# A hybrid attention layer in two halves of the tokens: top-k search and sparse attention of the second half placed beside the MLP of the first

## The chip, the cores and the metric

The kernel runs on one core of one Trainium2 chip. The metric is the device time of one execution in microseconds (us). Engines: PE is TensorE, DVE is VectorE, ACT is ScalarE, POOL is GpSimd; SP issues most of the DMAs.

## The reference

One layer over 1024 tokens of width 1024, all in float32. Two groups of heads read one projection; their outputs are normed, concatenated and projected, and an MLP follows.

```
mod = silu(c) @ w_mod + b_mod                    # six vectors sh1, sc1, ga1, sh2, sc2, ga2
h = rmsnorm(x, g_attn) * (1 + sc1) + sh1
proj = h @ w_in                                  # split into the parts below
o_a = stick_breaking_attention(q_a, k_a, v_a)    # 8 heads of 64, strictly causal
o_b = dsa_attention(...)                         # 8 heads over a shared latent of 128
x = x + ga1 * (concat(rmsnorm(o_a), rmsnorm(o_b)) @ w_out)
h = rmsnorm(x, g_mlp) * (1 + sc2) + sh2
x = x + ga2 * (square(relu(h @ w_up)) @ w_down)  # 1024 -> 4096 -> 1024
out = rmsnorm(x, g_final)
```

Stick-breaking weighs key s for query t by beta_ts times the product of (1 - beta_tj) over s < j < t, with beta a sigmoid of the scores. The sparse heads first score all admissible keys with an indexer (8 small heads, relu, weighted sum), keep the 256 best of each query, and take a softmax over these with a position bias. A query sees the keys of its own chunk of 64 and of earlier ones, so the first half of the tokens needs nothing of the second.

## The kernel before, in words

All tiles have 128 partitions; the tokens are 8 blocks of 128 (two halves of 4), and block b has 128 (b + 1) keys. Every float32 matmul of precision is done as three: each operand is split into a rounded high part and the rest (`split`, L155 to L160; for weights `load_split`, L162 to L175: DMA, scale by a gate on DVE in L172 where there is one, high part on ACT in L173, rest on POOL in L174), and `mm3` (L177) issues L178, L179 and L180 for it. Most PE work stands under these three lines, whatever it belongs to; the tile names tell it apart.

The program is written in one order, but each engine's queue is laid out before the run by a planner: it simulates the engines and takes, for each one, the ready instruction that comes first in the program (`early` moves a call up or down by the offsets in `PRI`), if a buffer of its pool is free. Buffers are named by tags with a count; a tile waits for the last reader of the one whose place it takes.

The stages, in program order:

- x is loaded, normed and transposed; the first modulation vectors come from w_mod (L289); h is made as 32 half tiles hh and hl in the pool `hpool`, which has 32 places (L314).
- The indexer (L430 to L467) leaves the scores sc of blocks 2 to 7. Blocks 0 and 1 have no more than 256 keys and need no search.
- The search finds the 256th largest score of each row bit by bit, 32 steps (L538). Blocks 2 to 6 step together on DVE: a count for each block (L503 on the upper 16 bits, L529 on the lower 16) and two small operations that close the step. Block 7 counts on ACT (Sign with a sum, L552), with two small operations on DVE. Then one mask per block (`topk_mask`, L561 to L582; five passes of its width, L578 to L582) is made in bfloat16.
- The stick-breaking heads run in four pairs, 8 steps a pair (L860): a step is one head and two blocks of queries. `sb_weights` (L698) makes scores (L380, L381), two Sigmoids (L707, L708), a scan on DVE (L709) and a product on POOL (L711). `av_pair` (L610) transposes the weights (L621, L623), copies and splits them (L626 to L632), multiplies them with the values (L644, 256 columns) and adds the two halves of the result (L662). In each step the lists TK, MS and DQ say how many search steps, modulation pieces (`mod_piece`, L388: weights of w_mod, one multiply-add on DVE each, L402) and halves of the projection dq (`dq_half`, L766) are put in; the search begins ahead of the first pair and all masks are done by the end of the last.
- The sparse heads (L1059): 8 heads by 4 pairs of blocks. `ds_weights` (L790) makes the logits dz with mm3 and adds the mask by a matmul (L809), reduces them with the bias on DVE (L812), takes Exp on ACT with a sum (L816), and scales by the reciprocal on ACT, POOL or DVE (L819, L821, L823). `ds_finish` is `av_pair` again. The norm of the stick-breaking output and part of that of the sparse one are put in between (L918 to L965).
- The output projection (`out_tile`, L982) has w_out whole in 16 tiles and runs token block by token block; `h2_pair` (L1005) makes the MLP's input h2h and h2l from two token blocks. Ten modulation pieces stand here too (`MW`).
- The MLP (L1106): 8 groups of 4 slices of w_up; for each slice both halves of the tokens go through `up` (24 matmuls of 512 columns per half), Relu on ACT (L1119), square on DVE (L1120) and split (L159, L160); then `dn` over the 8 token blocks and 2 column halves (12 matmuls each), added to x1 on DVE (L1138). The last group ends in the final norm (L1143 to L1150).

The two lines that count in the search, and the two activations of the two kinds of heads:

```
V.tensor_scalar(jk[:, :widths[b]], src or sc[b], t, 0.5 - TOPK, op0=op, op1=OP.add, accum_out=c)        # L503
V.tensor_scalar(jk[:, :widths[b]], mk[b].bitcast(U16), tlo[:, j:j + 1], above[:, j:j + 1],
                op0=OP.is_ge, op1=OP.add, accum_out=cnt[0][:, j:j + 1])                                 # L529
A.activation(m[:, cs], z, AF.Sigmoid, scale=-0.125)                                                     # L707
A.activation(l, l, AF.Exp, bias=mx, scale=-1.0, accum_out=st[:, 0:1])                                   # L816
```

Of the kernel before, what the change touches and what calls it, by code (L numbers as in the profile page):

```python
# [1 line left out]

# [16 lines left out]
P = 128  # L19
# [13 lines left out]
TKB = ((2, 3, 4, 5, 6), (7,))  # L33
TK0 = 1
OTB = 1
DEPTH = 2
TRB = 3
AVB = 1
ZB = 4
ZO = 1  # L40
NA = (0, 1)
DQ2 = [0] * 32
MACB = 2
KTG = ((0, 1), (1, 3), (3, 5), (5, 7), (7, 8))
PMK = ()
PRI = {'tk': 0, 'mod': -100, 'proj': 50, 'dq': 0, 'v': 100, 'sw': 0, 'sf': 400, 'dw': -200, 'df': 0, 'kv': -200, 'ld': 0, 'na': 0, 'wo': -50, 'vb': 0, 'mt': 0, 'ht': 0, 'fp': 0, 'pb': 0, 'h2': 0}
HFD = (6, 7)
HLD = ((0, 1), (2, 0), (2, 1), (3, 1), (4, 0), (4, 1), (5, 1), (7, 0))
IKD = ()
TRA = (4,)  # L50
WL = 4
WS = 4
QK = 6
VA = 5
WT = 4
KL = 3
WHB = 2
WLB = 2
WRB = 2
LPS = ((1, 0), (1, 2), (2, 2), (3, 4))  # L60
LPD = ()
AVL = 0
FPOS = 'wfvsdtm'
SBO = (2, 0, 3, 1)
DSO = (3, 2, 1, 0)
SCP = (2, 6)
OTP = False
WOR = (1, 3, 6, 7)
WOV = (0,)
MW = [6, 1, 1, 5]  # L70
WOA = ((7, 3, 0), (6, 3, 1), (6, 3, 2))
DSL = 0
NBK = 0
PS_ACT = (1, 2)
PS_POOL = (0, 2, 3, 5, 6, 7)
MI = [4, 0, 5, 0, 2, 0, 0, 5]
# [8 lines left out]
def tile_trunk(ctx: ExitStack, tc: tile.TileContext, x, w_mod, w_in, w_uv, w_out, w_up, w_down,  # L85
# [76 lines left out]
    def load_split(shape, src, name, hi_tag=None, lo_tag=None, raw_tag=None, scale=None, lo_eng=None):  # L162

        hp_, ht, hb = hi_tag or (wp, "wh", WHB)
        lp_, lt, lb = lo_tag or (wp, "wl", WLB)
        rp_, rt, rb_ = raw_tag or (wp, "wr", WRB)
# [24 lines left out]
    DVE_BLOCKS, ACT_BLOCKS = TKB  # L191
    hTh, hTl = {}, {}
    widths = {b: P * (b + 1) for b in range(NB)}
    with ExitStack() as pctx:
        bp = pctx.enter_context(tc.tile_pool(name="bpool", bufs=1))
        pp = pctx.enter_context(tc.tile_pool(name="psb", bufs=1, space=PSUM))

        def ztile(name):
            return pp.tile([P, 512], F32, tag="z", bufs=ZB, name=name)

        def pjtile(name):
            return pp.tile([P, 512], F32, tag="tr", bufs=TRB, name=name)

        def trtile(name):
            return pp.tile([P, 512], F32, tag="tr", bufs=TRB, name=name)

        def avtile(name):
            return pp.tile([P, 512], F32, tag="av", bufs=AVB, name=name)

        def big(name, dt=F32):  # L210
            return bp.tile([P, S], dt, tag="wkL", bufs=WL, name=name)

        def wktile(name, n):
            if n > 512:
                return big(name)
            return bp.tile([P, 512], F32, tag="wkS", bufs=WS, name=name)

        def qktile(name):
            return bp.tile([P, S], F32R, tag="qk", bufs=QK, name=name)

        def kltile(name):
            return bp.tile([P, S], F32R, tag="kl", bufs=KL, name=name)

        def vtile(name):
            return bp.tile([P, 2, 4, P], F32R, tag="va", bufs=VA, name=name)
# [20 lines left out]
        for tt in range(8):  # L246
            xt = big(f"x{tt}") if tt < 4 else bp.tile([P, S], F32, tag="va", bufs=VA, name=f"x{tt}")
# [16 lines left out]
        for hf in range(2):  # L264
            for t4 in range(4):
# [3 lines left out]
                jk = bp.tile([P, D], mybir.dt.uint8, tag="jka", bufs=1, name=f"xjk{tt}")  # L269
# [19 lines left out]
        def mod_tiles(k0, k1):  # L289
            n = k1 - k0  # L290
            acc = bp.tile([P, 2, n * P], F32, tag="wt", bufs=WT, name=f"macc{k0}")
            ps = trtile(f"pm{k0}")
            for k in range(KT):
                r = raws[k0, k][:, 0:2, :]
                if k0 in PMK:
                    continue
# [4 lines left out]
            for s_ in range(2):  # L301
                for j in range(n):
                    if k0 in PMK:
                        for k in range(KT):
                            T.matmul(ps[:, n * s_ + j:n * s_ + j + 1], raws[k0, k][:, s_, j * P:(j + 1) * P],
                                     c_act[:, k:k + 1], start=k == 0, stop=k == KT - 1)
                        continue
# [890 lines left out]
```

## Time and profile before

| | us |
|---|---|
| median of 3 runs | 1624.12 (1624.05 to 1626.75) |
| the profiled execution, its own time | 1625.42 |
| its span, first to last instruction | 1623.6 |
| mean granted clock of TensorE | 0.948 of full |
| PE, DVE, ACT, POOL busy | 1468.8, 990.5, 667.6, 567.5 |
| moved by DMA | 121.49 MB |

A row of a group reads: line, engine, operation, out<-in by the program's names (buffer numbers left out), shapes, count | busy us, mean ns of one | idle time of the engine just before these and what ended most of it. Matmuls are pipelined: the duration of one reaches into the next, so their mean is no price and a busy PE is not a full one. "+4 forms" says that shapes of other sizes are in the group. Stretches are us from the start of the span.

### The profile page before, as it was taken

The numbers are of one execution on the slowest core, as the hardware profiler recorded it, in microseconds if no ns is written. First come the engines' busy times: TensorE is split into PE (matmuls) and PEld (weight loads), VectorE is DVE, ScalarE is ACT, GpSimd is POOL, SyncE is SP. The second block draws the span as 40 slices with busy tenths as digits, with TensorE's granted clock in tenths as the row PEclk, the third lists the DMA queues.
The fourth block names the chain that finished last, engine by engine and source line by source line (L and its number), as shares of the span: only waits on it lengthen the run. The fifth ranks groups of instructions, "written<-read, shape, count | busy, mean of one in ns | idle before, by whom it ended". The sixth has DMA issues, their size and how long they took to land.

```text
span 1623.6 us, 19672 instructions
## 1 busy us (share of the span) xinstructions
PE 1468.8 (90%) x7248; PEld 1213.9 (75%) x7248; DVE 990.5 (61%) x1842; ACT 667.6 (41%) x1258; POOL 567.5 (35%) x389
## 2 busy tenths in 40 slices
PE   4888867887798778999999899999999999999998
PEld 3668746666587657878778688888888888888886
DVE  7888999999957885999763542323333332323234
ACT  5775565433445545988632330303031212212032
POOL 4343123433436556675552330403031222213021
PEclk8999979888899879999999999999999999999999
DMA  9531211322111212211342530202021111202012
GB/s 324 150 105 28 78 46 39 105 64 91 34 40 40 68 55 85 91 59 53 117 143 101 208 94 0 92 13 78 26 65 40 53 52 39 66 27 78 6 34 104
DMA packets 103232, 121.49 MB, mean 75 GB/s; under 512 B 7856, under 2 KB 75480, under 8 KB 103136
## 3 DMA queue, kind: packets, MB, share of 16 engines
q1 hardware_dynamic: 102704, 120.20, 23.7%
q8 instruction: 57, 0.93, 0.3%
q14 instruction: 39, 0.32, 0.1%
q10 hardware_dynamic: 432, 0.03, 0.0%
HBM read 99.75 MB, written 16.27 MB: 71 GB/s over the span
## 4 chain that ended last, share of the span: by engine, by line
PE 61%; DVE 27%; issue 4%; ACT 3%; DMA 3%; POOL 1%; SPq 0%; DVEq 0%; POOLq 0%; ACTq 0%
PE up L178 7%; PE up L180 7%; PE up L179 7%; PE dn L178 7%; PE dn L179 7%; PE dn L180 7%; DVE tk_jk L503 4%; DVE tk_jk L529 4%; DVE m L709 4%; DVE m2acc L402 2%; DMA wm<-in_w_mod_dram 2%; PE wo L178 2%; PE wo L179 1%; PE wo L180 1%; PE avd L644 1%
## 5 line engine op out<-in xcount | busy, mean ns | idle before, releaser
L174 POOL TENSOR_TENSOR wld<-wrd,whd 128x1024 fp32r<-128x1024 f32 x32 | 77.3, 2415 | 474.5 <-ACT whd L173 474.5
L1138 DVE TENSOR_TENSOR x<-dn,x 128x512 f32<-128x512 f32 x128 | 87.7, 691 | 206.7 <-PE dn L180 206.7
L1119 ACT ACTIVATE r<-up 128x512 f32<-128x512 f32 x64 | 37.8, 591 | 402.7 <-PE up L180 402.7
L178 PE MATMUL up<-h2h,whup 128*128 128x512 f32 x512 | 200.0, 391 | 3.2 <-ACT h2f L1020 3.2
L179 PE MATMUL up<-h2l,whup 128*128 128x512 f32 x512 | 199.7, 390 | 0.0
L180 PE MATMUL up<-h2h,wlup 128*128 128x512 f32 x512 | 199.7, 390 | 0.0
L179 PE MATMUL dn<-wld,uh 128*128 128x512 f32 x512 | 199.2, 389 | 0.0
L180 PE MATMUL dn<-whd,ul 128*128 128x512 f32 x512 | 199.2, 389 | 0.0
L178 PE MATMUL dn<-whd,uh 128*128 128x512 f32 x512 | 196.6, 389 | 0.0
L1120 DVE SCALAR_TENSOR_TENSOR r<-up,r 128x512 f32<-128x512 f32 x64 | 44.3, 692 | 196.7 <-ACT r L1119 196.7
L711 POOL TENSOR_TENSOR be<-be,m 128x895 f32<-128x895 f32 (+7 forms) x64 | 89.5, 1401 | 170.0 <-DVE m L709 114.8
L709 DVE TENSOR_TENSOR_SCAN m<-m 128x896 f32<-128x896 f32 (+7 forms) x64 | 98.7, 1548 | 27.7 <-ACT m L707 25.3
L178 PEld LDWEIGHTS up<-h2h,whup 128*128 128x128 f32 x512 | 96.5, 188 | 23.5 <-ACT h2f L1020 3.5
L179 PEld LDWEIGHTS up<-h2l,whup 128*128 128x128 f32 x512 | 96.5, 189 | 20.1
L180 PEld LDWEIGHTS up<-h2h,wlup 128*128 128x128 f32 x512 | 96.4, 188 | 20.1
L178 PEld LDWEIGHTS dn<-whd,uh 128*128 128x128 f32 x512 | 96.1, 188 | 20.0
L180 PEld LDWEIGHTS dn<-whd,ul 128*128 128x128 f32 x512 | 96.1, 188 | 20.0
L179 PEld LDWEIGHTS dn<-wld,uh 128*128 128x128 f32 x512 | 96.1, 188 | 19.9
L174 POOL TENSOR_TENSOR wlup<-wrup,whup 128x1024 fp32r<-128x1024 f32 x32 | 77.1, 2408 | 27.3 <-ACT whup L173 27.2
L160 DVE TENSOR_TENSOR ul<-r,uh 128x512 fp32r<-128x512 f32 x64 | 57.2, 894 | 44.7 <-ACT uh L159 44.7
L529 DVE TENSOR_SCALAR_CACHE_REDUCE tk_jk<-mk,tlo,above 128x384 bf16<-128x384 uint16 (+4 forms) x80 | 74.7, 933 | 2.0
L644 PE MATMUL avs<-wts,va 128*128 128x256 f32 (+1 forms) x320 | 56.5, 306 | 16.4 <-DVE ota L662 7.3
(328 smaller groups left out, 3705.5 us busy)
## 6 DMA issues: line engine op xcount, KB each, us to landing
m2raw<-in_w_mod_dram SPq DMA_DIRECT2D x32, 512.0 KB, 4.4
wrup<-in_w_up_dram SPq DMA_DIRECT2D x32, 512.0 KB, 3.9
wrd<-in_w_down_dram SPq DMA_DIRECT2D x32, 512.0 KB, 3.4
wm<-in_w_mod_dram SPq DMA_DIRECT2D x24, 256.0 KB, 6.0
x<-in_x_dram SPq DMA_DIRECT2D x8, 512.0 KB, 6.2
wrdq<-in_w_in_dram SPq DMA_DIRECT2D x8, 512.0 KB, 3.7
dq<-dqf SPq DMA_DIRECT2D x16, 256.0 KB, 2.2
dqr<-dq SPq DMA_DIRECT2D x8, 512.0 KB
```

What stands on the lines that cost most here:

```text
L160: (lo_eng or V).tensor_tensor(lo, src, hi.bitcast(F32), op=OP.subtract)
L174: (lo_eng or G).tensor_tensor(lo, raw, hi.bitcast(F32), op=OP.subtract)
L178: T.matmul(ps, ah, bh, start=start, stop=False)
L179: T.matmul(ps, ah, bl, start=False, stop=False)
L180: T.matmul(ps, al, bh, start=False, stop=stop)
L503: V.tensor_scalar(jk[:, :widths[b]], src or sc[b], t, 0.5 - TOPK, op0=op, op1=OP.add, accum_out=c)
L529: V.tensor_scalar(jk[:, :widths[b]], mk[b].bitcast(U16), tlo[:, j:j + 1], above[:, j:j + 1], op0=OP.is_ge, op1=OP.add, accum_out=cnt[0][:, ...
L644: T.matmul(dst, vv, rhs, start=kt == 0 and l == 0, stop=half and l == 1)
L709: V.tensor_tensor_scan(m[:, :n][:, ::-1], m[:, :n][:, ::-1], m[:, :n][:, ::-1], 1.0, op0=OP.mult, op1=OP.bypass)
L711: G.tensor_tensor(be[:, :n - 1], be[:, :n - 1], m[:, 1:n], op=OP.mult)
L1120: V.scalar_tensor_tensor(r, ps, 0.0, r, op0=OP.max, op1=OP.mult)
L1138: V.tensor_tensor(x1[tt][:, cs], ps, x1[tt][:, cs], op=OP.add)
```

## The change

The program order after the change: the indexer as before; then the search in two groups on DVE, blocks 2 and 3 first, then blocks 4, 5 and 6 (block 7 on ACT as before). While the stick-breaking heads run, the lists TK and TA put in 51 of the 71 steps of the two groups (all of the first, and 16 of the second) and the 32 bit steps of block 7. The projections dq and kv are all done in the first three pairs; in the last pair the sparse heads of the first half (blocks 0 to 3) are put in, by the list D0, two steps to each stick-breaking step, their tiles in the places that hh and hl leave. All modulation pieces are done by then. A new set of pools is opened, with 3 + 2 + 1 + 2 places in PSUM for scores, transposes, the weighted values and the MLP (before: 4 + 3 + 1). Then come the norm and output projection of the first half, and its MLP as a generator of 97 pieces: 2 of them, then one after each step left of the search, then four after each of 18 steps of the second half's sparse heads. Then the norm, output projection and MLP of the second half alone, with the up matmuls one group ahead of the down matmuls. The weights w_up, w_down, w_out and w_uv are loaded and split once for each half; in the first half's MLP w_down is split in pieces of 512 columns.

Its core:

```diff
-TKB = ((2, 3, 4, 5, 6), (7,))
...
-MS = [2, 0, 1, 2, 2, 1, 1, 1, 1, 1, 0, 1, 1, 0, 0, 0, 0, 0, 0, 0, 0, 0, 0, 0, 0, 0, 0, 0, 0, 0, 0, 0]
-DQ = [1, 1, 1, 1, 1, 2, 0, 2, 0, 1, 1, 1, 0, 0, 0, 0, 0, 0, 0, 0, 0, 0, 0, 1, 0, 0, 1, 0, 1, 0, 1, 0]
-TK = [1, 1, 2, 1, 1, 2, 0, 2, 2, 1, 4, 0, 4, 0, 2, 0, 1, 2, 4, 3, 0, 0, 1, 0, 2, 1, 1, 1, 0, 0, 0, 3]
+GROUPS = ((2, 3), (4, 5, 6))
+ACT_BLOCK = 7
...
+MS = [2, 0, 1, 2, 2, 1, 1, 1, 1, 1, 0, 1, 1, 0, 0, 0, 1, 0, 1, 0, 1, 0, 1, 0, 1, 1, 1, 1, 1, 1, 0, 0]
+DQ = [1, 1, 1, 1, 1, 2, 0, 2, 0, 1, 1, 1, 0, 0, 1, 1, 0, 0, 1, 1, 0, 0, 0, 0]
+TK = [2, 2, 2, 2, 2, 2, 2, 2, 2, 2, 2, 2, 2, 2, 2, 2, 2, 1, 1, 1, 1, 1, 1, 1, 1, 1, 1, 1, 1, 1, 1, 1]
+TA = [1] * 32
+D0 = [3, 2, 2, 2, 2, 2, 2, 3]
+FILL_0, FILL_T, FILL_D = 2, 1, 4
...
+        def ds_steps(hf):
...
+            yield first
+            for h in range(8):
+                for i in (2 * hf + 1, 2 * hf):
+                    yield lambda h=h, i=i: step(h, i)
+            yield lambda: [ds_finish(*t) for t in todo]
...
+        tk, ta = chain(*[search(g) for g in GROUPS]), search_act(ACT_BLOCK)
+        run(tk, 2)
...
+        d0 = ds_steps(0)
         for pr in range(4):
...
-                            early("tk", topk_some, TK[8 * pr + k])
+                            run(tk, TK[8 * pr + k])
+                            run(ta, TA[8 * pr + k])
...
+                    if pr == 3:
+                        run(d0, D0[k])
                     k += 1
         sb_finish(*pending)
-        topk_some(99)
-        while left() > 10:
+        run(d0, 99)
+        while left():
             mod_some(1)
...
+        pctx.close()
+        pctx = ExitStack()
+        bp = pctx.enter_context(tc.tile_pool(name="dpool", bufs=1, reuse_waits="tile"))
+        pp = pctx.enter_context(tc.tile_pool(name="psd", bufs=1, space=PSUM, reuse_waits="tile"))
...
+        def up_tile(ft, hf, ps, r, uh, ul, lo_eng=None):
+            wuh, wul = load_split([P, KT, P], wu[:, :, ft * P:(ft + 1) * P], f"up{ft}_{hf}")
+            for kt in range(KT):
+                mm3(ps, wuh[:, kt, :], wul[:, kt, :], h2h[kt, hf], h2l[kt, hf], kt == 0, kt == KT - 1)
+            A.activation(r, ps, AF.Relu)
+            V.scalar_tensor_tensor(r, ps, 0.0, r, op0=OP.max, op1=OP.mult)
+            split(uh, ul, r, None, lo_eng)
...
+            def dn(fg, t, ch):
+                ps = mtile(f"dn{fg}_{t}_{ch}")
+                ts = slice(t * P, (t + 1) * P)
+                for f in range(FFG):
+                    mm3(ps, uh[f][:, ts], ul[f][:, ts], *wd[f, ch], f == 0, f == FFG - 1)
+                V.tensor_tensor(x1[t, ch], ps, x1[t, ch], op=OP.add)
...
+            yield begin
+            for fg in range(NG):
+                for f in range(FFG):
+                    yield lambda fg=fg, f=f: up(fg, f)
+                for ch in range(2):
+                    for t in range(4):
+                        yield lambda fg=fg, t=t, ch=ch: dn(fg, t, ch)
+
+        norm(0, 0)
+        norm(0, 1)
+        out_half(0)
+        m = mlp_beside()
+        run(m, FILL_0)
+        for _ in range(40):
+            n0 = len(seen)
+            run(tk, 1)
+            run(ta, 1)
+            if len(seen) == n0:
+                break
+            run(m, FILL_T)
+        d = ds_steps(1)
+        for _ in range(18):
+            run(d, 1)
+            run(m, FILL_D)
+        norm(1, 0)
+        run(m, 200)
+        norm(1, 1)
+        out_half(1)
...
+        up_group(0)
+        for fg in range(NG):
+            if fg < NG - 1:
+                up_group(fg + 1)
```

`search` and `search_act` hold the operations of `topk_step` and `topk_mask` as generators, `run` takes the next steps of one, `norm` and `out_half` hold those of the norms and of `out_tile` for one half, and `up_group` calls `up_tile` for four slices of the second half.

## Rows read from the trace of the kernel before

**Rows 1.** The page, part 1: busy us of each engine, share of the span, instructions.
```profile
PE 1468.8 (90%) x7248; PEld 1213.9 (75%) x7248; DVE 990.5 (61%) x1842; ACT 667.6 (41%) x1258; POOL 567.5 (35%) x389
```

**Rows 2.** Busy time by stage: stretch, length, each engine's busy us (instructions), granted clock, DMA share, GB/s.
```profile
158.00:226.00 68.00, 55.16 (x271) 44.40 (x269) 66.80 (x176) 38.24 (x64) 11.65 (x5) 0.89 0.27 72
226.00:640.00 414.00, 336.29 (x1735) 278.81 (x1736) 354.44 (x575) 201.40 (x418) 183.57 (x117) 0.87 0.20 60
640.00:826.00 186.00, 172.12 (x1179) 147.72 (x1178) 155.55 (x516) 146.47 (x319) 116.26 (x86) 0.98 0.23 78
826.00:918.40 92.40, 85.63 (x398) 67.11 (x396) 46.44 (x90) 31.12 (x61) 34.19 (x42) 1.00 0.39 127
918.40:1623.60 705.20, 698.08 (x3072) 577.57 (x3072) 239.87 (x311) 149.13 (x222) 159.30 (x90) 1.00 0.18 58
```

**Rows 3.** The chain of waits, in order of time: start us, us, what.
```profile
670.46 1.50 PE avd L644 x12
...
860.13 1.31 PE x2T L1014 x12
```

**Rows 4.** Groups of PE from 226 to 640 us: count, busy us, mean ns, idle before.
```profile
L644 PE MATMUL avs<-wts,va 128*128 128x256 f32 (+1 forms) x292 | 52.7, 308 | 16.4 <-DVE ota L662 7.3 <-DVE wts L632 7.1 <-POOL wts L630 1.5
L178 PE MATMUL dq<-hh,whdq 128*128 128x512 f32 x120 | 50.5, 421 | 4.5 <-DVE qo L371 3.9 <-ACT wfs L629 0.4 <-DVE wts L632 0.2
...
L623 PE MATMUL trs<-ident,be 128*128 128x128 f32 x153 | 39.5, 309 | 2.7 <-POOL be L711 2.7
L621 PE MATMUL trs<-ident,be 128*128 128x128 f32 x123 | 36.3, 315 | 30.1 <-DVE modT L418 16.0 <-DVE wts L632 6.5 <-ACT wfs L629 5.4
L178 PE MATMUL k<-hh,whk 128*128 128x512 f32 x48 | 22.2, 463 | 1.0 <-ACT wfs L629 0.5 <-DVE lo L690 0.5
...
L178 PE MATMUL q<-hh,whq 128*128 128x512 f32 x40 | 16.9, 423 | 0.0
```

**Rows 5.** Groups of PE from 640 to 826 us.
```profile
L644 PE MATMUL avd<-wtd,vb 128*128 128x256 f32 (+1 forms) x317 | 47.9, 287 | 4.1 <-ACT wtd L626 2.2 <-DVE otb L662 1.1 <-DVE wtd L632 0.3
L178 PE MATMUL dz<-kvh,dqh 128*128 128x384 f32 (+4 forms) x94 | 37.8, 403 | 4.2 <-DVE dst L812 3.0 <-DVE dst L817 1.1
L623 PE MATMUL trd<-ident,dl 128*128 128x128 f32 x160 | 35.2, 274 | 0.0
L621 PE MATMUL trd<-ident,dl 128*128 128x128 f32 x128 | 33.0, 282 | 4.2 <-DVE wtd L632 3.1 <-DVE of L937 0.9
...
L178 PE MATMUL wo<-who,oh 128*128 128x512 f32 x24 | 9.9, 440 | 0.0
```

**Rows 6.** Busy time of two stretches of the stick-breaking stage, columns as in rows 2.
```profile
200.00:440.00 240.00, 184.99 (x848) 147.48 (x846) 235.36 (x484) 115.26 (x231) 78.18 (x51) 0.84 0.23 67
440.00:520.00 80.00, 71.68 (x459) 63.71 (x459) 52.06 (x70) 42.77 (x90) 40.35 (x24) 0.93 0.15 42
```

**Rows 7.** Groups of VectorE from 158 to 640 us.
```profile
L529 DVE TENSOR_SCALAR_CACHE_REDUCE tk_jk<-mk,tlo,above 128x384 bf16<-128x384 uint16 (+4 forms) x80 | 74.7, 933 | 2.0
...
L402 DVE SCALAR_TENSOR_TENSOR m2acc<-m2raw,c_act,m2acc 128x512 f32<-128x512 f32 x20 | 17.0, 848 | 0.0
L579 DVE TENSOR_TENSOR_SCAN cs<-eq 128x384 f32<-128x384 f32 (+5 forms) x6 | 13.3, 2210 | 2.8 <-POOL be L711 2.8
...
L581 DVE SCALAR_TENSOR_TENSOR cs<-sc,thr,cs 128x384 f32<-128x384 f32 (+5 forms) x6 | 8.1, 1342 | 0.1
L580 DVE SCALAR_TENSOR_TENSOR cs<-cs,cnt,eq 128x384 f32<-128x384 f32 (+5 forms) x6 | 7.8, 1308 | 0.1
L582 DVE TENSOR_SCALAR mk<-cs 128x384 bf16<-128x384 f32 (+5 forms) x6 | 7.2, 1194 | 0.0
L578 DVE TENSOR_SCALAR eq<-sc,thr 128x384 f32<-128x384 f32 (+5 forms) x6 | 6.7, 1122 | 0.0
```

**Rows 8.** ScalarE in order of time, 642 to 644 us.
```profile
642.40 1.28 ACT L816 ACT_TABLE_LOAD   x1
643.75 1.04 ACT L816 ACTIVATE dl<-dl,dst 128x896 f32<-128x896 f32 x1
```

More of the change, by code (lines that the diff above doesn't have):

```diff
@@ L1 @@
 from contextlib import ExitStack
+from itertools import chain
 import concourse.bass as bass
@@ L392, in mod_piece @@
             acc = macc2[c]
-            rp_, rt, rb_ = (bp, "va", VA) if c < 6 else (wp, "wr", WRB)
-            raw = rp_.tile([P, 2, 512], F32, tag=rt, bufs=rb_, name=f"m2raw{c}_{k2}")
-            SY.dma_start(raw, wm[:, 2 * k2:2 * k2 + 2, c0:c0 + 512])
+            if late:
+                raw = [hp.tile([P, 512], F32, tag="h", name=f"m2raw{c}_{k2}_{u}") for u in range(2)]
+                for u in range(2):
+                    SY.dma_start(raw[u], wm[:, 2 * k2 + u, c0:c0 + 512])
+            else:
+                both = bp.tile([P, 2, 512], F32, tag="va", bufs=bf["va"], name=f"m2raw{c}_{k2}")
+                SY.dma_start(both, wm[:, 2 * k2:2 * k2 + 2, c0:c0 + 512])
+                raw = [both[:, u, :] for u in range(2)]
             for u in range(2):
@@ L433, in tile_trunk @@
         done = []
+        late = []
         def left():
@@ L586, in tile_trunk, with run, htile @@
+        seen = []
+        def run(it, n):
+            for _ in range(n):
+                s_ = next(it, None)
+                if s_:
+                    seen.append(1)
+                    s_()
+        def htile(name, dt=F32R):
+            return hp.tile([P, 512], dt, tag="h", name=name)
         va = {}
@@ L883, in tile_trunk @@
                         elif what == "d":
-                            for _ in range(DQ[8 * pr + k]):
-                                n_ = next(dqi, None)
-                                if n_ is not None:
-                                    early("dq", dq_half, n_ // 2, n_ % 2)
-                    if pr == 3 and k in (2, 4):
-                        if k == 2:
+                            for _ in range(DQ[8 * pr + k] if pr < 3 else 0):
+                                q_ = next(dqi, None)
+                                if q_ is not None:
+                                    early("dq", dq_half, q_ // 2, q_ % 2)
@@ new lines, in tile_trunk, with norm @@
+        V.scalar_tensor_tensor(A2, modT[:, 32:40], 1.0, gmT, op0=OP.add, op1=OP.mult)
+        oh_, ol_, of_ = {}, {}, {}
+        def norm(hf, part):
+            kts = range(4 * part, 4 * part + 4)
+            sqs = []
+            for kt in kts:
+                of_[kt, hf] = htile(f"of{kt}_{hf}", F32)
+                SY.dma_start(of_[kt, hf], scr[kt][:, hf * 512:(hf + 1) * 512])
+                sq = wktile(f"sq{kt}_{hf}", 512) if kt % 4 else htile(f"sq{kt}_{hf}", F32)
+                A.activation(sq, of_[kt, hf], AF.Square)
+                if sqs:
+                    G.tensor_tensor(sqs[0], sqs[0], sq, op=OP.add)
+                else:
+                    sqs.append(sq)
+            st = bp.tile([P, 4], F32, tag="nst", bufs=2, name=f"nst{hf}_{part}")
+            row_rstd1(pjtile(f"ss{hf}_{part}"), sqs, 512, st)
+            rs = pjtile(f"rs{hf}_{part}")
+            row_rstd2(rs, 4, st)
+            for kt in kts:
@@ L1005, in h2_pair @@
+                split(oh_[kt, hf], ol_[kt, hf], raw, A, G)
+        h2h, h2l = {}, {}
         def h2_pair(i, xs):
@@ L1094, in tile_trunk @@
+        mctx.close()
     with ExitStack() as pctx:
```

680 lines of the change are left out of this document (294 added, 386 removed).

## The prediction

> **What bounds it now.** I read the page's first part, then busy time by stage, then the groups of instructions inside a stage, then the chain of waits, and last ScalarE's order of time around one spot. The first part says PE 90% [rows 1], which looks like a kernel with nothing left. The stages say otherwise [rows 2]. From 918.4 us on (the MLP), 3072 matmuls of 512 columns keep PE busy 698.1 us: 0.227 us each, back to back. Before that a busy PE is not a full one. The chain shows what the other kinds cost when nothing holds them: 12 matmuls of mostly 256 columns in 1.50 us (0.125 each), 12 transposes in 1.31 us (0.109 each) [rows 3]. With these prices I turn counts into dense PE time. For 226 to 640 us (stick-breaking heads): dq, k and q are 120 + 48 + 40 matmuls on each of the three lines of mm3, 624 x 0.227 = 142; avs 292, a fifth of them half as wide, 33; 153 + 123 transposes 30 [rows 4]; v, kv and the scores, counted in the same way, 71: 276 us of dense work in 414 us, 67%. For 640 to 826 us (sparse heads): avd 36, dz 3 x 94 of mean 384 columns (0.172) 48, 160 + 128 transposes 31, vb and masks 13, so 128, and 72 first wo matmuls 16 [rows 5]: about 148 in 186 us, 80%.
>
> What holds PE in the first stretch is VectorE: 235.4 of 240 us busy from 200 to 440 us, but 52.1 of 80 from 440 to 520 [rows 6], when the bit steps of the search have ended. So the search of blocks 2 to 6 sets the pace of half of the stick-breaking stage, and VectorE is idle two thirds of the MLP (239.9 of 705.2 us) [rows 2]. That imbalance is what the change goes at.
>
> **The change, part by part.** The sum is built from stage ends on the profiled execution (span 1623.6, its own time 1625.4, so 1.8 outside; the median of the runs shown is 1624.1, 1.3 below it).
>
> 1. Start to 226 us: the same work. 0.
>
> 2. Stick-breaking with the first half's sparse heads. Removed from VectorE: lower steps of blocks 4, 5, 6 (72% by width of the 74.7 us) 54; their accumulator reads and the two small operations that close a step, about 15; mask passes of blocks 4 to 7, 79% of 13.3 + 8.1 + 7.8 + 7.2 + 6.7 = 34; all of these [rows 7]; halving and the extra passes for block 7 about 13. That is 116 by single durations, which overlap a little in this stretch; I take 107. Added: two searches now close their steps separately, 22; the first half of the sparse heads, which by its tiles (3 of 10 transposed groups, 28% of the columns) is 30% of VectorE's 155.6 us [rows 2], 47; ten modulation pieces that stood in the output stage, 16 accumulations at 0.85, 13 [rows 7]. VectorE: 354 - 107 + 22 + 47 + 13 = 329. PE: 276 + 30% of 128 + 3 (vb is built for 12 groups instead of 8) = 317. Together 646. In the kernel before, PE's dense time plus VectorE's busy time was served at (276 + 354)/414 = 1.52 per us in the stick-breaking stretch and (148 + 156)/186 = 1.63 in the sparse one [rows 2]. Bounds: VectorE back to back, 329 (end at 555); the rate 1.52, 425 (end at 651). The mixed stage has work of both kinds, so I take 1.58: 409, end at 635.
>
> Then a cost that no row before has more than once: ScalarE's Sigmoid (L707, L708) and Exp (L816) now alternate in the last pair of heads. The order of time shows one change from Sigmoid to Exp, with a table load of 1.28 us, and 1.35 us from its start to that of the Exp behind it [rows 8]. There are 32 Exps in the half, so 2 to 64 loads, 3 to 86 us. One bundle of Exps per step of the stick-breaking heads is 8 x 2 = 16; I take 20, 27 us. ScalarE in that pair: a quarter of 201.4 is 50, 30% of 146.5 is 44 [rows 2], with the loads 121; at 90% busy 134, where PE and VectorE would need about 119. So 15 more: end at 650. The Trainium skill, page ScalarE: Activation LUTs, section What ACT_TABLE_LOAD costs, puts a switch at 1283 ns plus a drain of about 1380 ns, 2.66 us; this trace agrees on the load and not on the drain. By that figure the sum would be 20 x 1.31 / 0.9 = 29 us worse.
>
> 3. Norms and output projection of the first half: 192 matmuls 43.6, 32 transposes 3.5. Before, 312 and 64 of them (78 us) took 92.4 [rows 2], 14 lost; and now the norm of the b part cannot begin before the last sparse head: store, load, squares, adds, splits, some 14 more, which nothing covers on PE. 75, end at 725. Below it can hardly go (62 if the norm were covered), above it 90.
>
> 4. MLP of the first half beside the second half of the sparse heads: 349 (half of 698.1) + 70% of 128 + 2 = 441 dense. Bound above: the first 20 MLP pieces (7 up, 13 down: 73 us of PE) alternate with the rest of the search, and their evictions on VectorE are queued behind it: 107 and 20 of 192 such pieces' share of 239.9, 25, are 132 us of VectorE, so PE could lose 59. But stage 3 leaves VectorE more than half free, and the order is not the program's: 24 x 3 wo matmuls run before the last sparse head's end [rows 5]; so search steps, which need VectorE alone, can go ahead. I take 20 lost: 461, end at 1186. VectorE's 70% of 156 and half of 240 fit easily.
>
> 5. Second half's norms and output: as 3, but the a part's norm is done early and a few MLP pieces are left as cover: 60, end at 1246.
>
> 6. MLP of the second half: 349 + 6 (what stands now between last matmul and end) = 355, end at 1601. Weights of w_up, w_down and w_out are loaded and split twice, by their shapes 38 MB more. In the MLP now ScalarE is busy 149.1 and POOL 159.3 of 705.2 us, DMA 18% [rows 2]; the same in half the time is 42%, 46%, 36%. Costed at nothing; if a split came late, PE would stall at an up tile (5.4 us of matmuls each), at most a microsecond or two for 32.
>
> Sum: 226 + 424 + 75 + 461 + 60 + 355 = 1601, with 1.8 outside 1603 us: 1.3% faster.
>
> **The rivals.** (a) More is won. If the Exps come in few bundles and the search runs ahead, stage 2 runs at 1.63 without the ScalarE term (396, end at 622, 28 less) and stage 4 at its dense 441 (20 less): 1555. For it: the sparse stretch before ran all three engines above 78% busy [rows 2]. Against: the stick-breaking stretch did not, even with VectorE at two thirds [rows 6].
>
> (b) Slower: table loads make ScalarE the bound of the last pair of heads. At 64 loads it needs 94 + 86 = 180, at 90% 200 us instead of 134: 66 more, 1669. It decides from 34 loads on: 134 + 21 = 155 us, x 0.9 - 94 = 46, over 1.35; there the time is back at 1624. For it: Exps wait for VectorE's reductions and come when these are ready, not in bundles. Against: ScalarE waited much in this stretch (201.4 of 414) [rows 2]. The skill's rule to batch activations by table set (same page, section Table sets: the hidden batching unit) is broken by this change as in this rival; no run here shows it yet.
>
> (c) The search holds the MLP: stage 4 takes its upper bound, 39 more, 1642. It decides where less than a third of the 59 us is done ahead. Against: the scheduling ahead named above.
>
> (d) It doesn't do what it says: the two extra serial stretches (3 and 5) cost what the overlap gives, 1624.
>
> **How the numbers follow.** My case 0.44 (1575 to 1620), (a) 0.19, (b) 0.20, (c) 0.09, (d) 0.08. A measurement here can tell 0.2%, 3.2 us. Faster: my case nearly all, and (a), 0.62; same 0.07; slower 0.31. The range reaches down to (a), 1550, and up to half of (b) and all of (c), 1655; its own range for the likeliest case stands above.
>
> **What would show it.** Step 2: fewer DVE rows of the search before the first output projection, VectorE no longer full from 200 to 440 us, the last first-half avd near 650. Table loads: their count, 20 expected, over 34 is (b). Step 4: up and dn matmuls between dz and avd, PE near 0.227 us per matmul there; waits of up or dn on VectorE with search rows between are (c). Step 6: half the matmuls in 349 us without waits on weight splits. Wrong is the forecast if the first output projection starts after 690 us or stage 4 takes over 485.

## The result and the profile after

The changed kernel takes 1742.6 us (median of 4 runs, 1741.7 to 1745.5) against 1625.3 for the kernel before on the same chip: ratio 1.0725, 95% interval 1.0706 to 1.0743. It is 7% slower, and 140 us from the forecast, outside its range. The profiled execution has a span of 1740.4 us. Line numbers in the rows from here on are those of the changed kernel (L178 to L180, the three lines of `mm3`, are L155 to L157 there).

The first part of the page after (it answers to [rows 1]):

```profile
PE 1515.3 (87%) x7256; PEld 1246.8 (72%) x7256; DVE 1123.7 (65%) x1995; ACT 775.8 (45%) x1400; POOL 780.0 (45%) x512
```

Busy time by stage, with the columns of [rows 2], cut at the places that the forecast names: stick-breaking with the first half's sparse heads, the first output stage (norm and projection), the first half's MLP beside the rest, the second output stage, the second half's MLP.

```profile
0.00:226.00 226.00, 181.09 (x877) 147.52 (x878) 191.80 (x384) 144.22 (x251) 77.78 (x59) 0.89 0.44 131
226.00:706.50 480.50, 394.16 (x2093) 331.51 (x2091) 330.43 (x625) 272.72 (x566) 196.61 (x142) 0.86 0.22 65
706.50:799.40 92.90, 63.09 (x254) 48.03 (x253) 38.21 (x57) 31.55 (x56) 53.98 (x46) 0.81 0.42 145
799.40:1299.40 500.00, 466.28 (x2244) 383.77 (x2245) 353.67 (x696) 192.43 (x330) 229.66 (x142) 0.96 0.28 86
1299.40:1379.80 80.40, 60.35 (x259) 46.69 (x257) 36.53 (x60) 29.80 (x55) 47.35 (x48) 0.87 0.39 134
1379.80:1740.40 360.60, 350.37 (x1536) 289.29 (x1536) 173.08 (x177) 105.11 (x144) 174.58 (x78) 0.99 0.31 98
```

PE has the same work as before (7256 matmuls against 7248) and 46 us more of busy time, at a mean granted clock of 0.919 against 0.948; the other 70 us of the loss are idle PE. Set against the kernel before, the 117 us of span divide so:

| work | before | after | |
|---|---|---|---|
| stick-breaking and all sparse heads | 600 (226 to 826) | 480.5, and what stage 4 takes beyond half of the MLP before (352.6): 147.4 | +28 |
| norms and output projection | 92.4 | 92.9 + 80.4 | +81 |
| MLP | 705.2 | 352.6 + 360.6 | +8 |

The rows are cut by place in time: 72 of the 384 output matmuls of the kernel before ran ahead of 826 and so stand in its first row [rows 5]. The first row, where the overlap was to win, lost 28, and each of the two output stages cost nearly as much as the one before.

Three stretches of stage 2 show what was busy when:

```profile
226.00:360.00 134.00, 109.58 (x512) 89.89 (x511) 130.32 (x288) 64.65 (x131) 47.54 (x31) 0.86 0.23 63
360.00:560.00 200.00, 182.92 (x1055) 155.72 (x1053) 118.49 (x140) 101.11 (x213) 95.47 (x64) 0.97 0.26 76
560.00:712.00 152.00, 101.66 (x531) 85.90 (x530) 82.03 (x200) 108.38 (x225) 56.13 (x49) 0.71 0.17 54
```

First VectorE is full (130 of 134), then PE (183 of 200, VectorE 118), and in the last stretch nothing is: PE 102, VectorE 82, ScalarE 108 of 152. In the chain of waits of that last stretch (start us, us, what) one cause can be seen:

```profile
636.55 1.28 ACT dl L815 x5
637.83 0.02 issue
637.85 1.28 ACT L700
639.13 0.01 issue
639.15 0.28 ACT m L700
639.42 0.17 ACT be L701
639.59 0.02 issue
639.61 1.28 ACT L815
640.89 0.01 issue
640.90 0.60 ACT dl L815 x2
641.50 0.02 issue
641.52 1.28 ACT L700
```

The pieces of 1.28 us that name a line and no tile are table loads: Sigmoid (L700, L701) and Exp (L815) take turns, a few instructions at a time. ScalarE's groups of these loads, in the whole run:

```profile
L815 ACT ACT_TABLE_LOAD x10 | 12.8, 1283 | 0.2
L700 ACT ACT_TABLE_LOAD x8 | 10.3, 1283 | 0.1
L107 ACT ACT_TABLE_LOAD x1 | 1.3, 1283 | 2.1 <-issue 2.1
L701 ACT ACT_TABLE_LOAD x1 | 1.3, 1283 | 0.0
```

That is 20 (the kernel before has 2), 18 of them from the two kinds of heads taking turns. In stage 4 PE's waits from 800 to 960 us (engine, line, releaser: us, times, longest) are for VectorE, which still has the search to do:

```profile
PE dn L155 <- DVE x L1091: 12.5, 8, 3.9
PE dn L155 <- DVE r L1047: 9.2, 2, 5.3
PE up L155 <- DVE r L1047: 7.2, 4, 3.3
```

The search had stood still. Two groups of VectorE (min/median/max ns, first and last start): the pass that begins a group's lower half, and block 7's mask.

```profile
L508 DVE TENSOR_SCALAR_CACHE_REDUCE tk_ja<-mk,thi x5: 605/864/1133, 204.3 to 826.4; 128x384 bf16<-128x384 bf16 x1, 128x512 bf16<-128x512 bf16 x1, 128x640 bf16<-128x640 bf16 x1, 128x768 bf16<-128x768 bf16 x1
L561 DVE TENSOR_SCALAR nq<-sc,thr x1: 1754/1754/1754, 793.8 to 793.8; 128x1024 f32<-128x1024 f32 x1
```

The upper 16 steps ended at 355 us; the second group's lower half began at 810 and ended at 917. Every count writes its throwaway result into one buffer with one place (tag `jk`), and places go in program order. Block 7's mask stands ahead of those steps, and needs two of the four wide buffers (tag `wkL`), which the output projection's rows hold until 794.

### The profile page after: what moved, and what is told of

It reads as the page before. It is cut to its first block, busy times and chain, and to the rows that moved or that the text cites. A ratio compares the mean times of both kernels' runs of the same rounds, so it can differ in the third digit from the quotient of the medians.

```text
span 1740.4 us, 20514 instructions
## 1 busy us (share of the span) xinstructions
PE 1515.3 (87%) x7256; PEld 1246.8 (72%) x7256; DVE 1123.7 (65%) x1995; ACT 775.8 (45%) x1400; POOL 780.0 (45%) x512
## 4 chain that ended last, share of the span: by engine, by line
PE 53%; DVE 24%; DMA 6%; issue 6%; POOL 6%; ACT 5%; SPq 1%; DVEq 0%; POOLq 0%; ACTq 0%
PE en L157 3%; PE en L156 3%; PE en L155 3%; PE vp L155 3%; PE vp L156 3%; PE vp L157 3%; DVE tk_jk L519 3%; DVE tk_jk L488 3%; PE dn L155 3%; PE dn L156 3%; PE dn L157 3%; DVE m L702 3%; PE up L155 2%; PE up L157 2%; PE up L156 2%
## 5 line engine op out<-in xcount | busy, mean ns | idle before, releaser
L155 PE MATMUL dn<-whd,uh 128*128 128x512 f32 x256 | 107.0, 418 | 22.8 <-DVE x L1091 13.6
L155 PE MATMUL up<-h2h,whup 128*128 128x512 f32 x256 | 103.7, 406 | 10.4 <-DVE r L1047 7.2
L156 PE MATMUL up<-h2l,whup 128*128 128x512 f32 x256 | 102.7, 401 | 1.9 <-DVE h2l L137 1.9
L157 PE MATMUL up<-h2h,wlup 128*128 128x512 f32 x256 | 102.2, 399 | 0.0
L157 PE MATMUL en<-whe,vl 128*128 128x512 f32 x256 | 99.2, 389 | 3.1 <-DVE vl L137 3.1
L157 PE MATMUL dn<-whd,ul 128*128 128x512 f32 x256 | 101.9, 403 | 0.0
L155 PE MATMUL vp<-h2h,whup 128*128 128x512 f32 x256 | 100.3, 392 | 0.3 <-ACT h2f L996 0.3
L156 PE MATMUL vp<-h2l,whup 128*128 128x512 f32 x256 | 100.2, 392 | 0.0
L157 PE MATMUL vp<-h2h,wlup 128*128 128x512 f32 x256 | 100.0, 391 | 0.0
L155 PE MATMUL en<-whe,vh 128*128 128x512 f32 x256 | 99.6, 389 | 0.0
L156 PE MATMUL en<-wle,vh 128*128 128x512 f32 x256 | 99.6, 389 | 0.0
```

The costliest lines, as they stand in the source:

```text
L155: T.matmul(ps, ah, bh, start=start, stop=False)
L156: T.matmul(ps, ah, bl, start=False, stop=False)
L157: T.matmul(ps, al, bh, start=False, stop=stop)
```

## The experiments

All against the kernel before on the same chip in the same batch. The columns after the ratio are the start of the first output matmul (wo), of the first up matmul, of the last matmul of the first half's MLP or of the second half's sparse heads (whichever is later), of the first up matmul of the second half, and the span, all of the profiled run in us.

| run | us | ratio (95%) | first wo | first up | stage 4 ends | second up | span |
|---|---|---|---|---|---|---|---|
| changed kernel | 1742.6 | 1.0725 (1.0706 to 1.0743) | 723.3 | 799.4 | 1299.4 | 1379.8 | 1740.4 |
| e1_place | 1752.4 | 1.0751 (1.0720 to 1.0782) | 759.8 | 835.4 | 1309.3 | 1391.6 | 1749.4 |
| e2_noswitch | 1714.9 | 1.0521 (1.0489 to 1.0553) | 698.6 | 774.7 | 1272.5 | 1353.2 | 1711.8 |
| e3_after | 1724.7 | 1.0581 (1.0551 to 1.0612) | 707.9 | 783.3 | 1284.0 | 1365.6 | 1722.7 |
| e5_raw3 | 1748.3 | 1.0726 (1.0695 to 1.0757) | 729.9 | 809.3 | 1301.3 | 1386.8 | 1746.2 |
| e6_mlp_last | 1811.4 | 1.1139 (1.1116 to 1.1161) | 713.4 | 808.3 | 1363.3 | 1452.4 | 1810.5 |
| e7_spread | 1761.8 | 1.0834 (1.0808 to 1.0860) | 723.7 | 799.8 | 1322.7 | 1399.6 | 1757.3 |
| e8_low_on_vector | 1743.7 | 1.0723 (1.0701 to 1.0744) | 724.7 | 799.9 | 1295.7 | 1377.9 | 1741.4 |
| e9_all | 1748.2 | 1.0750 (1.0732 to 1.0768) | 745.0 | 824.1 | 1309.4 | 1388.0 | 1746.7 |
| e10_low_and_raw | 1748.0 | 1.0743 (1.0715 to 1.0772) | 729.5 | 808.1 | 1303.8 | 1385.2 | 1747.5 |
| e11_best | 1729.1 | 1.0635 (1.0611 to 1.0659) | 711.1 | 789.2 | 1285.0 | 1366.1 | 1727.0 |
| e12_short_search | 1717.4 | 1.0555 (1.0517 to 1.0593) | 717.4 | 793.3 | 1271.5 | 1353.1 | 1711.7 |
| e13_deeper | 1719.9 | 1.0584 (1.0524 to 1.0644) | 702.7 | 778.2 | 1280.8 | 1361.4 | 1722.0 |
| e14_after_noswitch | 1716.8 | 1.0565 (1.0534 to 1.0596) | 701.8 | 778.6 | 1276.6 | 1358.1 | 1715.3 |

**Was the search held by the throwaway buffer?** The counts of block 7's mask write into a buffer that the mask owns anyway.

```diff
-            jk = mp.tile([P, S], BF16, tag="jk", bufs=1, name=f"tk_jm{b}")
+            jk = cs if b == ACT_BLOCK else mp.tile([P, S], BF16, tag="jk", bufs=1, name=f"tk_jm{b}")
...
-                jk = mp.tile([P, S], BF16, tag="jk", bufs=1, name=f"tk_jn{b}")
+                jk = cs
```

> The one edit: the two counts in the mask of block 7 write their unused result into a tile of that mask and no longer into the tile jk that all counts of the search share. Theory place: jk has one place, given in program order; the mask of block 7 stands ahead of the lower half of the search and must wait for the wide tiles that the output projection holds, so the search stood still from 358 to 810 us with VectorE idle. Then the lower steps now begin near 360, most are over before the first output projection ends, and stage 4 (first up matmul to last down matmul, 799 to 1300 in the changed kernel) shrinks by 40 to 60 us; the whole time falls to 1680 to 1705. Rival order: the planner takes nothing of the search across the change of pools or over so many instructions. Then the lower steps still begin near 800 and the time stays within 5 us of 1743.

The hold is shown: the counts of the lower half (L519) now all lie in the stick-breaking stage.

```profile
L519 DVE TENSOR_SCALAR_CACHE_REDUCE tk_jk<-mk,tlo,above x80: 644/939/1206, 209.6 to 475.9; 128x384 bf16<-128x384 uint16 x16, 128x512 bf16<-128x512 uint16 x16, 128x640 bf16<-128x640 uint16 x16, 128x768 bf16<-128x768 uint16 x16
```

Busy time of e1_place from 360 to 560 us:

```profile
360.00:560.00 200.00, 164.71 (x868) 138.59 (x866) 169.08 (x253) 80.85 (x169) 71.94 (x49) 0.87 0.21 61
```

The hope was wrong. From 360 to 560 us VectorE went from 118 to 169 busy, and PE from 1055 matmuls to 868. Stage 4 shrank from 500 to 474, and the first wo came 36 us later (2 more table loads, 22, are a small part of that); the whole can't be told from the changed kernel (1.0751 and 1.0725). VectorE's idle third there was no free place: from 360 to 560 us PE waited 23 us for results of VectorE, 12 in the changed kernel, and its granted clock was 0.87 instead of 0.97.

**What do the table loads cost?** Sigmoid in place of Exp in the first half's sparse heads (so their weights are not the softmax's).

```diff
-                A.activation(l, l, AF.Exp, bias=mx, scale=-1.0, accum_out=st[:, 0:1])
+                A.activation(l, l, AF.Exp if b > 3 else AF.Sigmoid, bias=mx, scale=-1.0, accum_out=st[:, 0:1])
```

> The first half's sparse heads take Sigmoid in place of Exp (their weights are then not the reference's); nothing else. No table load is left between 540 and 712 us (17 there now). Theory loads: the loads stand in the chain of the last pair, so the first half's last avd, at 700 us now, comes 20 to 35 us earlier and the time falls by as much, to 1708 to 1723. Rival chain: the stretch is bound by the waits of two interleaved chains for one another's buffers, and the loads lie beside them: under 8 us.

18 loads fewer, and the first output matmul comes 24.7 us earlier: 1.37 us a load, the whole distance from the start of a load to that of the next instruction, 1.35 [rows 8]. So on the average a load cost its full length; ScalarE's idle time covered nothing of it.

**Does mixing pay at all?** The first half's sparse heads behind the stick-breaking heads, and then the same without switches.

```diff
-D0 = [3, 2, 2, 2, 2, 2, 2, 3]
+D0 = [0, 0, 0, 0, 0, 0, 0, 0]
```

> D0 is all zeros: the first half's sparse heads come behind the stick-breaking heads instead of into their last pair. Theory loads and chain alike: the stick-breaking heads then end near 640 and the sparse ones need some 55 to 65 us alone (30% of 186), so the output projection begins near 700 as before and the time is within 15 us of 1743; two table loads are left. If mixing was worth anything at all, it is slower by 20 us or more; if mixing itself was the loss, it is faster by 20 us or more.

> Sigmoid in place of Exp in the first half's sparse heads (which leaves the table loads out; the weights of these heads are then not the reference's) and, as in e3_after, these heads behind the stick-breaking heads. e2_noswitch alone was 32 us under the changed kernel, e3_after, which also has 12 loads fewer, 22. Theory "the loads are all that mixing costs": without loads it makes no difference where the heads stand, or mixing even helps: 1711 to 1725, no better than e2_noswitch (1714.9). Rival "mixing costs by itself": 8 to 20 us under e2_noswitch, 1695 to 1707.

Unmixed, 8 of the 20 loads are left (more than the 2 expected in this stretch), and stage 2 is 15.4 us shorter: 12 loads at 1.28 us. By itself e3_after (18 us faster by the medians, 23 by the ratios, with 20 as the mark for "mixing itself was the loss") doesn't tell the loads from the mixing; e14_after_noswitch does. With no switch in either order it makes no difference where these heads stand: 1.0521 mixed, 1.0565 unmixed, first wo at 698.6 and 701.8. The mixing brought some 3 us by the first wo, less than the ratios can tell, and cost its switches. The heads by themselves, in e3_after, and the heads of both halves together, in the kernel before:

```profile
621.00:693.00 72.00, 48.51 (x272) 41.07 (x272) 36.76 (x144) 43.00 (x115) 21.14 (x21) 0.86 0.27 81
```

```profile
656.00:790.00 134.00, 124.92 (x904) 107.63 (x902) 123.93 (x431) 117.49 (x256) 85.11 (x61) 1.00 0.22 73
```

Both halves together keep PE at 93% with 904 matmuls in 134 us, 0.148 each; the first half's short rows alone get to 67%, 0.265 each. At the pace of before, 272 matmuls would take 40 us, not 72, if their kinds were mixed as before; the granted clock, 0.86 against 1.00, is a part of the difference.

**Is it the number of row blocks in flight?**

```diff
-                if len(todo) > DEPTH:
+                if len(todo) > (DEPTH if hf else 4):
```

> e3_after (the first half's sparse heads behind the stick-breaking heads, 1724.7) with four pairs of row blocks in flight in these heads instead of two. There PE was busy 48.5 of 72 us (621 to 693) at a clock of 0.86, with 272 matmuls, while the kernel before, with both halves' heads together, was busy 124.9 of 134 us with 904. Theory "the short rows' chain of small steps is what the time is" (each pair passes PE, VectorE, ScalarE, VectorE, PE, ScalarE, VectorE, PE in turn, and nothing else is there to fill PE): with more pairs in flight the 72 us fall to 52 to 64, the time to 1705 to 1717. Rival "not the depth" (one place for the accumulator of a pair and two heads' operands loaded at a time hold it): within 4 us of 1724.7.

The first output matmul comes 5.2 us earlier and more matmuls fall into the same 72 us (316), but the ratios, 1.0584 and 1.0581, can't be told apart. Depth is at most a small part of it. PE's longest waits in these 72 us are now for VectorE to empty the accumulator (`otd`, 13.2 us; 8.7 in e3_after), which has one place, as the rival said. But it has one place in the kernel before too, so what holds these heads stays open.

**Does standing beside the MLP give anything?** The MLP written behind the search and the second half's sparse heads (and the second norm's first part behind the MLP).

```diff
-FILL_0, FILL_T, FILL_D = 2, 1, 4
+FILL_0, FILL_T, FILL_D = 0, 0, 0
...
-        norm(1, 0)
         run(m, 200)
+        norm(1, 0)
```

> The first half's MLP written behind the search and the second half's sparse heads in the program (the second norm's first part behind the MLP), so that only what the planner itself moves forward stands beside them. Theory "standing beside gives what idle PE it fills": the search's end (some 100 us with PE otherwise idle) is then filled less, the stage from the end of the first output projection to the last down-projection grows from 500 by 40 to 80 us, and the time to 1780 to 1825. Rival "beside gives nothing, PE's own work bounds the stage either way": within 10 us of 1742.6.

```profile
800.00:880.00 80.00, 20.47 (x68) 14.81 (x68) 77.20 (x144) 4.88 (x6) 10.32 (x6) 0.61 0.17 55
```

Here PE is busy 20 of 80 us while VectorE searches; in the changed kernel it was 64. The ratio rises by 0.041, 67 us. Of the 70 us of span, 55 are in stage 4; some 9 in the second output stage may come from the norm, which was moved too. So standing beside does fill PE. But the gap that it fills is the new order's own: in the kernel before the search stood beside the stick-breaking heads, with PE busy 185 of 240 us [rows 6].

**Does the search hold the MLP?** Once by spreading it in the program, once by leaving most of its lower steps out.

```diff
-FILL_0, FILL_T, FILL_D = 2, 1, 4
+FILL_0, FILL_T, FILL_D = 2, 3, 2
```

> Three pieces of the MLP after each step of the search instead of one (and two instead of four after each step of the second half's sparse heads), so that the search stands more thinly at the start of the stage. Theory "the search holds the MLP" (rival c of the prediction): between 800 and 960 us PE was busy for 129 us of 160 and VectorE for 154; with the search spread out PE is busy for 145 or more of the same 160 us, the stage from the first up-projection to the last down-projection shrinks from 500 to 475 to 485 us, and the time falls by 15 to 25, to 1718 to 1728. Rival "the VectorE work is there wherever it is put": PE gains in the first 160 us and loses as much among the sparse heads, the stage stays within 495 to 505, and the time within 5 us of 1742.6.

```diff
-                yield lambda i=i: lower_step(i)
+                yield lambda i=i: lower_step(i) if i in (15, 0) else None
```

> Leaves out 14 of the 16 steps of the lower half of each search over blocks 2 to 6, so the masks of the sparse attention are those of a coarser threshold; everything else is computed, and each step's place in the program is kept. That takes 42 counts of 1.07 us and 14 pairs of small steps of 0.85 us, about 60 us, from VectorE at the head of the stage of the MLP, and some 35 us earlier, around 210 to 265 us. Theory "the search holds the MLP" (rival c): PE, which was busy 129 of the first 160 us of the stage at a clock of 0.89, is busy for 145 or more, and the stage from first up-projection to last down-projection falls from 500 to 465 to 475. Rival "the stage is PE's own work": it falls by 10 at most. The first group's steps may give up to 20 more in the stick-breaking stage; so 1690 to 1715 by the theory, 1712 to 1740 by the rival.

Busy time from 800 to 960 us, in the changed kernel in two parts, then e7_spread in the same two, then e12_short_search:

```profile
800.00:880.00 80.00, 64.20 (x236) 49.60 (x235) 76.19 (x133) 18.35 (x28) 32.48 (x21) 0.85 0.27 83
880.00:960.00 80.00, 64.93 (x272) 50.72 (x271) 78.27 (x131) 21.62 (x34) 29.64 (x17) 0.94 0.25 73
```

```profile
800.00:880.00 80.00, 64.53 (x232) 49.84 (x233) 75.96 (x133) 18.31 (x28) 31.74 (x21) 0.84 0.26 83
880.00:960.00 80.00, 59.70 (x237) 45.43 (x236) 75.84 (x117) 17.52 (x27) 27.13 (x15) 0.94 0.22 68
```

```profile
800.00:960.00 160.00, 145.95 (x646) 118.44 (x645) 116.08 (x189) 50.38 (x80) 72.17 (x41) 0.94 0.28 86
```

The spreading tested nothing of the search: it is ready, so the planner puts it at the head of VectorE's queue as before (76 of 80). What it did was to move MLP ahead of the second half's sparse heads: these end at 1322.7, 26 us after the last down-projection, with no MLP beside them (PE busy 18 of these 26 us), and the span rises by 17. Both expectations were wrong. Leaving the steps out answers the question in part: PE goes from 129 to 146 of the 160 us and stage 4 from 500 to 478, less than the theory's 25 to 35 and more than the rival's 10. These 14 steps cost 22 us of stage 4; the other 6 of the gain lie ahead of the first wo. The masks and the other two steps still stand there.

**What paces the output stages?** Their chain of waits is a loop of DMA, VectorE, ScalarE and POOL (`wlo`), with POOL's low parts of the normed rows (`ol`) between. One turn of it in the first output stage of the changed kernel:

```profile
731.08 2.67 DMA wro<-in_w_out_dram
...
733.84 1.62 DVE wro L149
735.49 0.64 ACT who L150
...
736.20 1.29 POOL wlo L151
```

So: three places for the raw weights (in BUFS2, against one of the bias tile), low parts on VectorE, and both.

```diff
-"nb": 2, "wr2": 2
+"nb": 1, "wr2": 3
```

> Raw pieces of w_out and w_down get 3 places instead of 2 (paid for by one place less for the bias tile nb). Theory raw: the output projections, some 88 and 80 us against 62 of work, are paced by two raw places, each through load, scale, high part and rest before the next load may start; then each becomes 8 to 15 us shorter and the time falls to 1715 to 1728. Rival: POOL's rests and the norm ahead of them set the pace; under 6 us.

```diff
-                              (bp, "wr2", bf["wr2"]), gate[:, cs])
+                              (bp, "wr2", bf["wr2"]), gate[:, cs], V)
```

> The low part of each of the output projection's weights on VectorE instead of POOL, for both halves. Theory "POOL paces the output stages" (its low parts take 1.3 us each and stand with its 1.5 us low parts of the normed rows, and PE waited 8.7 us for them in each stage): first output matmul to first up-projection falls from 76 to 64 to 70 us, last down-projection to the first up-projection of the second half from 80 to 68 to 74, and the time by 12 to 24, to 1719 to 1731. Rival "the weights' DMA paces them" (VectorE waited 35.1 us for it in the first of the two): both stages stay within 3 us, and the time within 5 us of 1742.6.

> Both edits of the output stage at once: the low parts of its weights on VectorE (as in e8_low_on_vector) and three places for the raw weights (as in e5_raw3, with one for the bias tile). Theory "two limits of the same pace": a piece of the weights goes DMA 2.6 us, VectorE 0.7, ScalarE 0.6, low part 0.7 to 1.3, and the next may use its place only then, which with two places is 2.3 to 2.7 us to a piece; POOL by itself is also 1.3 us a piece and as much for each low part of the normed rows. Either edit alone left the other limit, so both together shorten each output stage by 6 to 12 us: last down-projection to the first up-projection of the second half from 80 to 68 to 74, and the time falls by 10 to 25, to 1718 to 1733. Rival "neither sets the stage" (the norm's chain of small steps and the clock that falls with it do): within 5 us of 1742.6.

None shortens a stage by more than 1 us (first wo to first up 76.1, then 79.4, 75.2 and 78.6; second output stage 80.4, then 85.5, 82.2 and 81.4). The place taken from the bias tile in e5_raw3 and e10_low_and_raw may hide a gain of theirs; no run took the two apart. In e8_low_on_vector the chain in the second output stage goes on without POOL:

```profile
1317.84 3.03 DMA wro<-in_w_out_dram
...
1320.96 0.70 DVE wro L149
...
1321.74 0.64 ACT who L150
...
1322.41 0.69 DVE wlo L151
...
1323.13 2.98 DMA wro<-in_w_out_dram
```

One piece still takes 5.3 us from load to load, with two pieces under way. With both edits it is no faster either. The name in the chain changes and the stage stays, so POOL's low parts, which the chain named, were not its cause; what is stays open.

**All that had seemed to help, together.** e9_all: e3, block 7's mask in the last step of the stick-breaking loop (`TA = [1] * 31 + [2]`), e8 and e7. e11_best: e3, e5 and e8.

> All that was found at once: the first half's sparse heads behind the stick-breaking heads (as in e3_after, -22), block 7's mask in the last step of the stick-breaking loop (so that the other blocks' lower steps are not held behind it), the low parts of the output weights on VectorE, and the MLP spread three pieces to a step of the search. Theory "the gains are separate": 1742.6 - 22 - 18 - 20 = about 1683, with 1665 to 1700. Rival "displaced" (what e1_place showed: search that is taken ahead puts off as much stick-breaking work): no better than e3_after by more than 10 us, 1710 to 1730. Neither expects it under the kernel before (1624).

> The edits that gained or did no harm: the first half's sparse heads behind the stick-breaking heads (-22 alone), and both edits of the output stage. If these are separate and e10_low_and_raw gains, 1742.6 - 22 - 10 to 25 = 1696 to 1711; if it does not, 1716 to 1724. No theory has it under the kernel before (1624): the stages it leaves are 226, then 395 of stick-breaking, 87 of sparse heads, two output stages of 70 to 80 each, 485 to 500 of the MLP with the rest, and 360.

e9_all is worse than either theory had it. Against e3_after its first wo comes 37 us later: the lower counts now run up to 724 us, among the heads, and it seems that they put these off as in e1_place; 13 us of that come back later. e11_best is no better than e3_after either. No version came near the kernel before, so none is offered in its place.

## Why the prediction was wrong, step by step

Span times, forecast against measured; the errors add up to 139, the whole miss against the forecast span of 1601.

| step | forecast | measured | error |
|---|---|---|---|
| 1 start | 226 | 226 (the cut) | 0 |
| 2 stick-breaking and first sparse heads | 424 | 480.5 | +56 |
| 3 first output stage | 75 | 92.9 | +18 |
| 4 MLP beside the rest | 461 | 500.0 | +39 |
| 5 second output stage | 60 | 80.4 | +20 |
| 6 second MLP | 355 | 360.6 | +6 |

**Step 2: the counts were right, the rate and a price were wrong.** VectorE was forecast at 329 us and measured at 330.4; 20 table loads were forecast, 18 came. What failed first is "The mixed stage has work of both kinds, so I take 1.58". Without these loads (e2_noswitch, where first wo is 24.7 earlier, so the stage is 456 us) the same 646 us of work went at 1.42 per us, below both rates of the trace before. A sum of two engines' work over the time holds only while both have work ready. Here the search ran first, alone at the bound, then PE, then neither. That costs 47 us (456 less 409). The windows of e3_after and of the kernel before suggest why: the sparse stretch had got its 1.63 with the long rows of the second half in it, which were now elsewhere. No run shows it by itself, and the granted clock was not taken apart from it: 0.71 in the last of the three stretches, 0.86 in e3_after's heads, 0.98 in the sparse stretch before [rows 2]. (By its own terms, 128 and 16, the forecast's dense work there is 144 us and not 148, so 1.61 and not 1.63; that changes little.) The price is the second failure: loads were charged as a share of ScalarE, 15 us for 20. ScalarE had room (busy 108 of 152 us), but the loads stand in a chain through the engines, and the 18 cost 24.7. The Trainium skill, page ScalarE: Activation LUTs, section Table sets: the hidden batching unit, asks to batch activations by table set; e2_noswitch and e3_after agree, with 1.37 and 1.28 us won for each switch taken away. Rival (b) named the loads, but with ScalarE as the bound, from 34 loads on; with ScalarE not the bound, 18 cost more than the 22 us of gain forecast.

**Step 4: rival (c), in part.** "so search steps, which need VectorE alone, can go ahead" failed: a buffer with one place and an order of the program held them until 810 us, and the stage took 500, the forecast's own upper bound. The loss lies in the first 160 us. After them PE is full, at full clock (columns as above):

```profile
960.00:1300.00 340.00, 337.15 (x1744) 283.50 (x1743) 199.20 (x433) 152.46 (x269) 167.99 (x107) 1.00 0.30 90
```

From 800 to 960 us there are 508 matmuls, by the forecast's 0.227 each an estimated 115 us, so some 45 us were lost where it had put 20: 25 of the 39 us of error. Most of the other 14 is dense work counted short: 115 and 337 are 452, against 441. Leaving out 14 of the lower steps gave 22 us back (e12_short_search), and having all lower steps ahead of the stage 26 (e1_place). What is lost beyond that no run took apart: in both runs it lies in the first 80 us of the stage, where PE was busy 65 and 66 us at a granted clock of 0.84 and 0.88, with the masks still on VectorE. So the search was the largest part shown of the 45, not all of it. And where the steps did go ahead, stage 2 paid (e1_place).

**Steps 3 and 5: rival (d), at twice its size.** Forecast were 135 us for the two stages against 92.4 before, measured 173. Of step 3, the norm's uncovered chain was about right (16.8 us from the end of the last head to the first wo, 14 forecast); the projection behind it took 76 instead of 61. Each of w_out's pieces now feeds 12 matmuls where it fed 24, and they are loaded and split twice; what paces these stages stayed open above. The granted clock was 0.81 and 0.87 in them, 1.00 in the one before [rows 2]. Step 5 counted on cover, an early norm and MLP pieces left over, that was not there: all 97 pieces are out when the stage begins, and the factors of both parts of its norm are made only in it (from 1302 and 1328 us).

**Step 6 was right**, with double loading and splitting of the weights at nothing.

The forecast's own marks for being wrong (first output projection after 690, stage 4 over 485) both came: 723 and 500.

## What to carry to other kernels

Before moving work beside a PE-bound stage, ask what it stood beside until now: here the two halves' sparse heads had filled each other's waits at 93% PE, and the half left behind ran at 67%. A stage cut in two halves loads the same weights twice and gives each piece half the matmuls, and both halves need a cover of their own: here each cost nearly the whole (92.9 and 80.4 us, against 92.4). A table switch inside a chain of small steps can cost its full length, as it did here with ScalarE idle for 44 of 152 us. And an engine's idle third is not a free place for long instructions where another engine waits for its short ones.

## What the runs showed of the hardware

The Exp behind a table load starts at once (load at 639.61 for 1.28 us, Exp at 640.90 in the chain above), and 0.02 us lie between the Sigmoid ahead of it and the load. The drain of about 1380 ns that the Trainium skill gives on the page ScalarE: Activation LUTs, section What ACT_TABLE_LOAD costs, shows neither in that row nor in the 1.37 us that a load cost in e2_noswitch.

The first output stage opens with PE at 1.2 GHz, after waits of the norm and of the first weights, whose load took 8.13 us behind the stage's other loads. In the 12 us ahead of it PE was busy for 4.3. Busy time around it:

```profile
700.00:712.00 12.00, 4.27 (x20) 3.33 (x18) 1.81 (x4) 4.42 (x10) 4.74 (x4) 0.64 0.22 84
712.00:720.00 8.00, 3.30 (x14) 3.22 (x15) 0.16 (x1) 0.63 (x1) 2.28 (x2) 0.50 1.00 359
720.00:740.00 20.00, 15.59 (x58) 11.56 (x56) 7.87 (x9) 8.00 (x13) 15.94 (x12) 0.78 0.46 148
```

A granted clock of 0.50 is the lower of the two levels. So this serial stretch cost twice: PE idled in it, and the matmuls behind it began at half speed, the slowest of the wo matmuls with 796 ns against a median of 394.
